# Half rows behind the scores, early splits at the half switch, and M1 in two parts: a hybrid trunk layer on one core

## The chip, the cores and the metric

The kernel runs on one core of one Trainium2 chip. The metric is the device time of one launch in microseconds, given as the median of several runs. Beside it stands one profiled execution, from which all rows below come; their times count from the start of its span.

## What is computed

One layer of a diffusion trunk over 1024 tokens of width 1024, with 256 context tokens that only serve as keys and values. All in fp32:

- a modulation vector `mod = silu(c) @ w_mod + b_mod`, six pieces of 1024: shift, scale and gate of either half layer (`sh1, sc1, g1, sh2, sc2, g2`);
- `h = rms_norm(x) * (1 + sc1) + sh1`, then `h @ w_in`, from which three head groups are made: a chunked gated MLP, attention with 8 query heads over 2 key/value heads (normalised, rotated, 1280 keys), and a gated short convolution;
- `x = x + g1 * (concat(groups) @ w_out)`;
- `x = x + g2 * conv_ffn(rms_norm(x) * (1 + sc2) + sh2)`, where `conv_ffn` is `up = dwconv3(h @ w_up)` (2 × 2816 wide), `silu(g) * a`, and `@ w_down`;
- the output is `rms_norm(x)` times `final_g`.

## The kernel before

Every large product is done on pairs: a number is split into an upper part (`hi`, rounded to fp32r by ScalarE) and a lower part (`lo`, what is left, by VectorE), and three products hi·hi, hi·lo, lo·hi stand for one. A split is therefore one cast on ScalarE and one subtraction on VectorE. A recording layer with engine wrappers makes every instruction, so all of them have one line (L94) in the profile; tiles tell them apart. SP's DMAs keep their written order. The other engines' queues are ordered by a scheduler where `order("")` stands, and as written for the engines named, as `order("TVSG")` in the attention and `order("VS")` at the half switch.

**Attention.** Sixteen units (8 token blocks × 2 key/value heads) are run by a table `PROG`: `a`, `b` are the score products (tile `sl`, two buffers of two PSUM banks), `e` the exponentials on ScalarE, `T` the transpositions of the probabilities (tile `tr`, two banks), `K` and `L` their split (`ph` on ScalarE, `pw` on VectorE), `A` the products with V (`acc`), `f` the copy `sh` on ScalarE, once per unit. Beside it GpSimd multiplies `w_mod` by `silu(c)` for `sh2` and `sc2` and adds up (`mod_macs`, tile `mac`, two buffers, one for each half row of 512 columns). When a half row is done, `head` (L989) lets TensorE sum it over the partitions by four products with `ones` into a `tr` bank, and `tail` (L996) adds the bias on VectorE; both are put into the unit's program at `L8` and `L9`. From unit 16 on, products of the output projection (`po`, `o_early`, L1055) fill TensorE while the last units drain.

**Output projection and the ramp.** For each token block `o_mm` adds the projection to `x1`, `stats2` takes the square sum on ScalarE and `r` by a power on GpSimd and small steps on VectorE, `norm2` makes `xh`. `h_first(kb)` (L1233) transposes `xh` of the first 512 tokens (tile `p2_0*`), ScalarE applies scale and shift (`raw0`), and splits follow (`HB11`, `HB21`). `HF` (L37) says behind which block of the second half which of the eight `kb` are done. The up projection is a Strassen scheme on pairs of weight columns: seven products M1 to M7 on sums of quarter blocks (`HB`, `HT`). `RAMP` (L30) is the written order of its start: M parts of pairs 0 to 2, `H` (transpositions of the second 512 tokens, `p2_1*`), `C` and `F` (the sums), `S` (quarters of M6 and M5).

**Down projection.** It runs over the first 512 tokens, then over the second. For each of 22 `j` one load of gated rows `g` and weights `wd` is split (`d_load`, L1528) and 24 products go to eight `pd` banks. At the half switch `evac` (L1568) multiplies a bank by `g2` on VectorE and GpSimd adds it to `x1`. `final` (L1574) makes the output of a first-half token block at j = 3, 5, 7, 9 of the second half; its two output DMAs stand on SP in front of the next loads. `final_half` (L1586) makes the last block's output in two halves.

## Time and profile before

| | |
|---|---|
| median of 3 runs | 1292.92 us (1291.63 to 1293.93) |
| profiled execution | 1291.2 us, span 1289.4 us |
| mean granted TensorE clock | 0.990 |
| TensorE busy | 1240.2 us, 96% of the span |
| VectorE, ScalarE, GpSimd busy | 955.2, 622.1, 499.3 us |

The busy shares are means over stages with different limits. A row of the timeline gives the start, the duration, the engine, the output and input tiles (numbers left out), how many instructions were merged, and in brackets the idle time before it with what ended that. In the windows view the figure behind the busy times is the granted clock: 1.00 is the 2.4 GHz level, 0.50 the 1.2 GHz level. PE is TensorE, PEld its weight loads, DVE VectorE, ACT ScalarE, POOL GpSimd.

### The profile page before, as it was taken

The numbers are of one execution on the slowest core, as the hardware profiler recorded it, in microseconds if no ns is written. First come the engines' busy times: TensorE is split into PE (matmuls) and PEld (weight loads), VectorE is DVE, ScalarE is ACT, GpSimd is POOL, SyncE is SP. The second block draws the span as 40 slices with busy tenths as digits, with TensorE's granted clock in tenths as the row PEclk, the third lists the DMA queues.
The fourth block names the chain that finished last, engine by engine and source line by source line (L and its number), as shares of the span: only waits on it lengthen the run. The fifth ranks groups of instructions, "written<-read, shape, count | busy, mean of one in ns | idle before, by whom it ended". The sixth has DMA issues, their size and how long they took to land.

```text
span 1289.4 us, 17828 instructions
## 1 busy us (share of the span) xinstructions
PE 1240.2 (96%) x6420; PEld 1031.0 (80%) x6420; DVE 955.2 (74%) x1686; ACT 622.1 (48%) x1126; POOL 499.3 (39%) x497
## 2 busy tenths in 40 slices
PE   6989999999999999999999999999999999999997
PEld 3879899877777778787688888888888888878785
DVE  4797878379899896556999999997778765234545
ACT  4762233368788786225744444444434544122331
POOL 1252243069889855342145453454354110030001
PEclk9999999999999999999999999999999999999999
DMA  9906011111111000811123343333221358023741
GB/s 289 286 18 197 25 34 44 40 50 34 34 65 51 17 2 1 279 70 79 33 82 110 104 131 98 99 114 93 86 83 54 110 211 343 1 98 131 267 173 65
DMA packets 109189, 132.13 MB, mean 102 GB/s; under 512 B 7632, under 2 KB 77998, under 8 KB 109102
## 3 DMA queue, kind: packets, MB, share of 16 engines
q1 hardware_dynamic: 109102, 131.01, 30.9%
q8 instruction: 50, 0.82, 0.3%
q14 instruction: 37, 0.30, 0.1%
HBM read 111.07 MB, written 19.92 MB: 102 GB/s over the span
## 4 chain that ended last, share of the span: by engine, by line
PE 46%; DVE 3%; DMA 2%; ACT 1%; issue 1%; POOL 0%; SPq 0%; POOLq 0%; ACTq 0%; DVEq 0%
PE pd L94 14%; PE pY L94 14%; PE pZ L94 9%; PE pX L94 8%; DMA wd<-in_ffn_down 2%; DVE wd L94 1%; DVE HB L94 1%; DVE x1r L94 1%; SPq L107 0%; DMA x1d<-x 0%; ACT wd L94 0%; ACT HT L94 0%; DMA g<-gud 0%; DVE t_fin L94 0%; DVE xh L94 0%
## 5 line engine op out<-in xcount | busy, mean ns | idle before, releaser
L94 PE MATMUL pd<-wd,gt 128*128 128x512 f32 x912 | 208.4, 390 | 5.1 <-DVE wd L94 4.7
L94 PEld LDWEIGHTS pd<-wd,gt 128*128 128x128 f32 x912 | 171.0, 188 | 42.0 <-DVE wd L94 5.8
L94 PE MATMUL pY<-HT,wM 128*128 128x512 f32 x792 | 192.8, 392 | 2.8 <-ACT HT L94 2.2
L94 PEld LDWEIGHTS pY<-HT,wM 128*128 128x128 f32 x792 | 148.7, 188 | 35.9 <-ACT HT L94 3.3
L94 DVE TENSOR_TENSOR wM<-wu,wM 128x512 fp32r<-128x512 f32 x132 | 133.1, 1012 | 13.7 <-ACT wM L94 13.3
L94 ACT CAST wM<-wu 128x512 fp32r<-128x512 f32 x132 | 80.7, 620 | 114.0 <-PE pY L94 57.2
L94 PE MATMUL pX<-HB,wM 128*128 128x512 f32 x528 | 127.0, 389 | 0.0
L94 DVE TENSOR_TENSOR pw<-tr,ph 128x512 fp32r<-128x512 f32 x160 | 108.2, 682 | 13.0 <-ACT ph L94 11.9
L94 ACT CAST ph<-tr 128x512 fp32r<-128x512 f32 x160 | 93.6, 587 | 47.2 <-PE tr L94 46.0
L94 PEld LDWEIGHTS pX<-HB,wM 128*128 128x128 f32 x528 | 99.0, 188 | 20.4
L94 POOL TENSOR_TENSOR wu<-S,wu 128x512 f32<-128x512 f32 x22 | 29.1, 1322 | 176.5 <-DVE wM L94 176.3
L94 PE MATMUL sl<-K,Q 128*128 128x512 f32 x256 | 83.4, 420 | 1.7 <-ACT pp L94 1.7
L94 DVE TENSOR_REDUCE sm<-sl 128x1 f32<-128x1024 f32 x64 | 77.7, 1216 | 5.3 <-PE sl L94 5.2
L94 PE MATMUL tr<-ident,pp 128*128 128x128 f32 x512 | 78.1, 275 | 1.4
L94 POOL TENSOR_SCALAR pp<-pp,sm 128x1024 f32<-128x1024 f32 x64 | 71.7, 1127 | 17.3 <-DVE sm L94 17.3
L94 PEld LDWEIGHTS tr<-ident,pp 128*128 128x128 f32 x512 | 59.6, 140 | 21.9 <-DVE pw L94 15.5
L94 ACT CAST gt<-g 128x512 fp32r<-128x512 f32 x38 | 23.5, 619 | 110.6 <-DMA g<-gud 79.7
L94 ACT ACTIVATE pp<-sl,sm 128x1024 f32<-128x1024 f32 x64 | 71.5, 1117 | 4.8 <-DVE sm L94 3.8
L94 DVE TENSOR_TENSOR gt<-g,gt 128x512 fp32r<-128x512 f32 x38 | 26.1, 687 | 58.1 <-ACT gt L94 58.1
L94 DVE TENSOR_TENSOR wd<-wd,wd 128x1024 fp32r<-128x1024 f32 x44 | 55.7, 1266 | 17.3 <-ACT wd L94 15.3
L94 PE MATMUL pZ<-HT,wM 128*128 128x512 f32 x264 | 65.1, 393 | 0.3 <-ACT HT L94 0.3
L94 PE MATMUL pZ<-HB,wM 128*128 128x512 f32 x264 | 64.3, 392 | 0.0
(347 smaller groups left out, 2780.5 us busy)
## 6 DMA issues: line engine op xcount, KB each, us to landing
wu<-in_ffn_up SPq DMA_DIRECT2D x88, 256.0 KB, 3.2
wd<-in_ffn_down SPq DMA_DIRECT2D x44, 512.0 KB, 7.4
w<-in_w_mod SPq DMA_DIRECT2D x24, 512.0 KB, 3.7
g<-gud SPq DMA_DIRECT2D x44, 256.0 KB, 5.1
wm<-in_w_mod SPq DMA_DIRECT2D x16, 512.0 KB, 4.6
wi<-in_w_in SPq DMA_DIRECT2D x16, 512.0 KB, 4.7
gud<-y SPq DMA_DIRECT2D x11, 512.0 KB
gud<-ya SPq DMA_DIRECT2D x11, 512.0 KB
```

The lines of the kernel that those rows point to most:

```text
L94: i = fn(*a, **k)
```

## The change

- The 16 products that sum `mac` over the partitions and the four additions behind them are taken out of the attention loop. One `mod_heads` at the start of unit 16 does all 16 products into one `sl` buffer and one addition. `mac` has four buffers.
- `HF` moves each transposition of the first tokens behind a later token block; the last stands behind block 7.
- `RAMP` cuts M1 of pairs 0 and 1 in two parts, as that of pair 2 was, and puts the second parts behind `H0`.
- The first two loads and splits of the second half are written in front of the last `evac` of the first.
- In `final_half` VectorE, not GpSimd, multiplies the first half by `final_g`, the first half's square sum goes into the mean before the second is there, and the two output DMAs are issued by ScalarE and SP.

```diff
@@ -27,14 +27,14 @@
 GLAG = 6
 FINJ = (3, 5, 7, 9)
 GW0 = 4
-RAMP = "M1_0 M1_1 M1_2a H0 M1_2b C0 H1 C1 M2_0 F0 S0 H2 C2 F1 S1 M2_1 H3 C3 S2 S3 M7_0 M7_1 F2 F3"
+RAMP = "M1_0a M1_1a M1_2a H0 M1_0b M1_1b M1_2b C0 H1 C1 M2_0 F0 S0 H2 C2 F1 S1 M2_1 H3 C3 S2 S3 M7_0 M7_1 F2 F3"
 KB = 8
 DFF = 2816
 NF = DFF // P
 QD = 1
 NQ = 1
 PST = 3
-HF = ((0, 1), (2, 3, 4), (5, 6, 7), ())
+HF = ((), (0, 1, 2), (3, 4, 5, 6), (7,))
 SIDE = {2: "a00", 3: "a01", 4: "a20", 5: "a21", 6: "l0", 7: "l1", 8: "w000", 9: "w001",
         10: "w010", 11: "w011", 12: "l2", 13: "l3", 15: "w020"}
 MACS = ("y0", "y1", "z2", "g0")
@@ -143,12 +143,12 @@
     mhalf = const.tile([P, 16], F32, name="mhalf")
     G.memset(mhalf, -0.5)
 
-    def rstd_gen(ss, n, width, pl, name, eng=V):
+    def rstd_gen(ss, n, width, pl, name, eng=V, eps=EPS):
         v = pl.tile([P, width], F32, name=f"v_{name}", tag="rs_v", bufs=4)
         y = pl.tile([P, width], F32, name=f"y_{name}", tag="rs_y", bufs=4)
         t = pl.tile([P, width], F32, name=f"t_{name}", tag="rs_t", bufs=4)
         r = pl.tile([P, width], F32, name=f"r_{name}", tag="rs_r", bufs=4)
-        eng.tensor_scalar(v, ss, 1.0 / n, EPS, ALU.mult, ALU.add)
+        eng.tensor_scalar(v, ss, 1.0 / n, eps, ALU.mult, ALU.add)
         G.tensor_tensor(y, v, mhalf[:, 0:width], ALU.pow)
         yield r
         eng.tensor_tensor(t, v, y, ALU.mult)
@@ -976,7 +976,20 @@
             wos[i] = kq(f"wos{i}", [P, 2, 2, 512])
         fn(wos[i][:, 0, kk, :], wos[i][:, 1, kk, :], wol[i][:, kk, :])
 
-    heads, tails = [], []
+    macc2 = []
+
+    def mod_heads():
+        psb["b1"] = (pst, "sl", 2)
+        pm_ = b1("pm2")
+        for i, ac in enumerate(macc2):
+            for q in range(4):
+                c0 = 8 * i + 2 * q
+                T.matmul(pm_[:, c0:c0 + 2], ac[:, q * P:(q + 1) * P], ones,
+                         start=True, stop=True)
+        b0 = rows["bm"] + 24
+        V.tensor_tensor(mod2[:, 1:3, :].rearrange("p j k -> p (j k)"),
+                        pm_[:, 0:32].rearrange("p (q t) -> p q t", t=2)[:, :, 0],
+                        vT[:, b0:b0 + 16], ALU.add)
 
     def mod_macs(js, acc):
         def load(i):
@@ -985,19 +998,6 @@
             c0 = (2 + j) * D + half * 512
             dma(w_, w_mod[q * 256:(q + 1) * 256, c0:c0 + 512]
                 .rearrange("(k p) n -> p k n", p=P))
-
-        def head(j, half, ac):
-            pm_ = b1(f"pm2_{j}{half}")
-            for q in range(4):
-                T.matmul(pm_[:, 2 * q:2 * q + 2], ac[:, q * P:(q + 1) * P], ones,
-                         start=True, stop=True)
-            tails.append(lambda: tail(j, half, pm_))
-
-        def tail(j, half, pm_):
-            b0 = rows["bm"] + 16 + 8 * j + 4 * half
-            V.tensor_tensor(mod2[:, j, 4 * half:4 * half + 4],
-                            pm_[:, 0:8].rearrange("p (q t) -> p q t", t=2)[:, :, 0],
-                            vT[:, b0:b0 + 4], ALU.add)
 
         ld = {}
         idx = [8 * (j - 1) + i for j in js for i in range(8)]
@@ -1007,6 +1007,7 @@
             j, half, q = i // 8 + 1, i // 4 % 2, i % 4
             if q == 0:
                 ac = acc(f"mac{j}{half}")
+                macc2.append(ac)
             for kk in range(2):
                 k, w_ = 2 * q + kk, ld[i][:, kk, :]
                 G.tensor_scalar(w_ if k else ac, w_, scT[:, k, 0:1], 1.0, ALU.mult, ALU.mult)
@@ -1016,8 +1017,6 @@
                 if kk and n + 2 < len(idx):
                     load(idx[n + 2])
                 yield
-            if q == 3:
-                heads.append(lambda j=j, half=half, ac=ac: head(j, half, ac))
 
     def side(words):
         for w in words.split():
@@ -1125,16 +1124,14 @@
                 sc_, pl = scores(u_ // 2, u_ % 2)
                 us[u_] = {**sc_, **av(u_ // 2, u_ % 2, pl)}
             o, k, l = prog[at]
-            if (o, k) == ("L", 9) and tails:
-                tails.pop(0)()
+            if n == 16 * len(prog):
+                mod_heads()
             if 0 <= u_ - l < 16 and not (u_ == l and o in ops0):
                 us[u_ - l][o](k)
             if u_ == 1 and at == 0:
                 make_gB0()
                 macs = mod_macs((1, 2), lambda nm: tp.tile([P, 512], F32, name=nm, tag="mac",
-                                                              bufs=2))
-            if (o, k) == ("L", 8) and heads and u_ < 16:
-                heads.pop(0)()
+                                                              bufs=4))
             if o + str(k) in MACS:
                 for _ in range(3 if o == "g" and SIDE.get(u_, "l")[0] == "l" else 1):
                     next(macs, None)
@@ -1539,6 +1536,17 @@
     def wd_tile(j, hf):
         return mx(f"wd{j}{hf}", [P, 2, 1024])
 
+    def d_load1(j):
+        if j < NF - LATE:
+            gt = w4(f"gt{j}1", [P, 2, 512])
+        else:
+            if (j - NF + LATE) % 2 == 0:
+                g2.append(ex(f"gl{j}", [P, 2, 2, 512]))
+            gt = g2[-1][:, (j - NF + LATE) % 2]
+        return d_load(j, 1, gt, wd_tile(j, 1))
+
+    g2 = []
+
     def d_load0(j):
         return d_load(j, 0, w4(f"gt{j}0", [P, 2, 512]), wd_tile(j, 0))
 
@@ -1587,16 +1595,18 @@
         sl = x1(7)[:, cs]
         if n2 == 0:
             S.activation(jo[:, 1, cs], sl, AF.Square, accum_out=ss7[:, 0:1])
-            G.tensor_tensor(sl, sl, fg[:, cs], ALU.mult)
+            V.tensor_tensor(sl, sl, fg[:, cs], ALU.mult)
+            V.tensor_scalar(ss7[:, 2:3], ss7[:, 0:1], 1.0 / D, EPS, ALU.mult, ALU.add)
             return
         V.scalar_tensor_tensor(jo[:, 1, cs], sl, 1.0, sl, ALU.mult, ALU.mult,
                                accum_out=ss7[:, 1:2])
-        V.tensor_tensor(ss7[:, 2:3], ss7[:, 0:1], ss7[:, 1:2], ALU.add)
-        r = rstd_from(ss7[:, 2:3], D, 1, xf, "fin7")
+        g = rstd_gen(ss7[:, 1:2], D, 1, xf, "fin7", V, ss7[:, 2:3])
+        r = next(g)
+        next(g, None)
         V.scalar_tensor_tensor(sl, sl, r, fg[:, cs], ALU.mult, ALU.mult)
         S.activation(x1(7)[:, 0:512], x1(7)[:, 0:512], AF.Copy, scale=r)
-        for q in range(2):
-            dma(out[7 * P:8 * P, q * 512:(q + 1) * 512], x1(7)[:, q * 512:(q + 1) * 512])
+        nc.scalar.dma_start(out[7 * P:8 * P, 0:512], x1(7)[:, 0:512])
+        dma(out[7 * P:8 * P, 512:1024], x1(7)[:, 512:1024])
 
     BOTH = [(i, n2) for i in range(4) for n2 in range(2)]
 
@@ -1628,19 +1638,16 @@
             fg = jo[:, 0, :]
             dma(fg, final_g.partition_broadcast(P))
     order("VS")
+    nxt1 = []
     for i, n2 in BOTH:
         for k, ts in enumerate(last):
             d_mm(NF - 4 + k, i, n2, ts)
+        if (i, n2) == (3, 1):
+            nxt1 += [d_load1(0), d_load1(1)]
         evac(i, n2)
     late = []
     for j in range(NF):
-        if j < NF - LATE:
-            gt = w4(f"gt{j}1", [P, 2, 512])
-        else:
-            if (j - NF + LATE) % 2 == 0:
-                g2 = ex(f"gl{j}", [P, 2, 2, 512])
-            gt = g2[:, (j - NF + LATE) % 2]
-        ts = d_load(j, 1, gt, wd_tile(j, 1))
+        ts = nxt1[j] if j < len(nxt1) else d_load1(j)
         if j in FINJ:
             final(FINJ.index(j))
         if j < NF - LATE:
```

On TensorE, where the attention drains (`tr706` transposes probabilities of unit 14, `po00` is the first output projection), stood before:

```order
L94 MATMUL tr706_6171<-ident_67,pp700_5878 128x128 x2
L94 MATMUL tr706_6171<-ident_67,pp702_5973 128x128 x2
L94 MATMUL po00_6182<-wos0_4773,acm00_3591 128x512 x2
L94 MATMUL po00_6182<-wos0_4773,acm01_3592 128x512
L94 MATMUL acc70_6107<-ph704_6146,V_625 128x512
L94 MATMUL acc70_6107<-pw704_6167,V_625 128x512
```

and stands now:

```order
L94 MATMUL tr706_6147<-ident_67,pp700_5855 128x128 x2
L94 MATMUL tr706_6147<-ident_67,pp702_5949 128x128 x2
L94 MATMUL pm2_6158<-ones_96,mac10_3330 128x2 x4
L94 MATMUL pm2_6158<-ones_96,mac11_3921 128x2 x4
L94 MATMUL pm2_6158<-ones_96,mac20_4562 128x2 x4
L94 MATMUL pm2_6158<-ones_96,mac21_5202 128x2 x4
L94 MATMUL po00_6176<-wos0_4761,acm00_3591 128x512 x2
L94 MATMUL po00_6176<-wos0_4761,acm01_3592 128x512
```

All sixteen `pm2` products stand between `tr706` and `po00`.

On TensorE at the start of the ramp (`p2_07` is the last transposition of the first tokens, `p2_10` the first of the second, `pX0` to `pX2` hold M1 of pairs 0 to 2, `po17` before them is the projection of block 7) stood before:

```order
L94 MATMUL pX0_7154<-HB11_0_6954,wM1_0_6744 128x512 x6
L94 MATMUL pX0_7154<-HB11_2_7029,wM1_0_6744 128x512 x6
L94 MATMUL pX1_7169<-HB11_0_6954,wM1_1_6835 128x512 x6
L94 MATMUL pX1_7169<-HB11_2_7029,wM1_1_6835 128x512 x6
L94 MATMUL pX2_7184<-HB11_0_6954,wM1_2_7032 128x512 x6
L94 MATMUL p2_10_7194<-ident_67,xh10_7144 128x128 x2
L94 MATMUL p2_10_7194<-ident_67,xh11_7145 128x128 x2
L94 MATMUL p2_11_7200<-ident_67,xh10_7144 128x128 x2
L94 MATMUL p2_11_7200<-ident_67,xh11_7145 128x128 x2
L94 MATMUL pX2_7184<-HB11_2_7029,wM1_2_7032 128x512 x6
L94 MATMUL p2_12_7231<-ident_67,xh10_7144 128x128 x2
L94 MATMUL p2_12_7231<-ident_67,xh11_7145 128x128 x2
```

and stands now:

```order
L94 MATMUL p2_07_7130<-ident_67,xh01_6892 128x128 x2
L94 MATMUL pX0_7148<-HB11_0_6988,wM1_0_6738 128x512 x6
L94 MATMUL pX1_7155<-HB11_0_6988,wM1_1_6829 128x512 x6
L94 MATMUL pX2_7162<-HB11_0_6988,wM1_2_7008 128x512 x6
L94 MATMUL p2_10_7172<-ident_67,xh10_7138 128x128 x2
L94 MATMUL p2_10_7172<-ident_67,xh11_7139 128x128 x2
L94 MATMUL p2_11_7178<-ident_67,xh10_7138 128x128 x2
L94 MATMUL p2_11_7178<-ident_67,xh11_7139 128x128 x2
L94 MATMUL pX0_7148<-HB11_2_7070,wM1_0_6738 128x512 x6
L94 MATMUL pX1_7155<-HB11_2_7070,wM1_1_6829 128x512 x6
L94 MATMUL pX2_7162<-HB11_2_7070,wM1_2_7008 128x512 x6
L94 MATMUL p2_12_7225<-ident_67,xh10_7138 128x128 x2
```

M1's six products on `HB11_2` of pairs 0 and 1 have moved behind `p2_10` and `p2_11`.

On VectorE at the half switch (`ev` are the evacuations, `gt` and `wd` the lower parts of the splits of the second half) stood before:

```order
L94 TENSOR_TENSOR ev30_11093<-pd30_10405,gacc0_7968 128x512
L94 TENSOR_TENSOR ev31_11108<-pd31_10412,gacc1_8539 128x512
L94 TENSOR_TENSOR gt01_11111<-g01_11113,gt01_11111 128x512
L94 TENSOR_TENSOR wd01_11112<-wd01_11117,wd01_11112 128x1024
L94 TENSOR_TENSOR gt11_11153<-g11_11155,gt11_11153 128x512
L94 TENSOR_TENSOR wd11_11154<-wd11_11159,wd11_11154 128x1024
L94 TENSOR_TENSOR gt21_11187<-g21_11189,gt21_11187 128x512
```

and stands now:

```order
L94 TENSOR_TENSOR ev30_11087<-pd30_10399,gacc0_7962 128x512
L94 TENSOR_TENSOR gt01_11102<-g01_11104,gt01_11102 128x512
L94 TENSOR_TENSOR wd01_11103<-wd01_11108,wd01_11103 128x1024
L94 TENSOR_TENSOR gt11_11112<-g11_11114,gt11_11112 128x512
L94 TENSOR_TENSOR wd11_11113<-wd11_11118,wd11_11113 128x1024
L94 TENSOR_TENSOR ev31_11122<-pd31_10406,gacc1_8533 128x512
L94 TENSOR_TENSOR gt21_11181<-g21_11183,gt21_11181 128x512
```

`ev31` has moved behind the splits of j = 0 and 1.

## Rows read from the trace of the kernel before

**Rows 1.** The page, part 1: busy us (share of the span) and instructions.

```profile
PE 1240.2 (96%) x6420; PEld 1031.0 (80%) x6420; DVE 955.2 (74%) x1686; ACT 622.1 (48%) x1126; POOL 499.3 (39%) x497
```

**Rows 2.** TensorE's waits: tile, releaser, us in total, times, longest.

```profile
PE pm L94 <- DVE pw L94: 5.4, 4, 1.4
...
PE pd L94 <- DVE wd L94: 4.7, 3, 3.2
```

**Rows 3.** Timeline of ScalarE, the copy that each attention unit makes once.

```profile
315.76 0.58 ACT L94 COPY sh<-acc 64x512 f32<-64x512 f32 x1
...
394.03 0.58 ACT L94 COPY sh<-acc 64x512 f32<-64x512 f32 x1
...
408.47 0.58 ACT L94 COPY sh<-acc 64x512 f32<-64x512 f32 x1
...
486.90 0.58 ACT L94 COPY sh<-acc 64x512 f32<-64x512 f32 x1
```

**Rows 4.** Timeline of TensorE at the first of the four sums.

```profile
328.46 1.05 PE L94 MATMUL pm<-ones,mac 128*128 128x2 f32 x8 [1.28 <-DVE pw L94]
329.37 0.71 PE L94 MATMUL sl<-K,Q 128*128 128x512 f32 x2
```

**Rows 5.** Windows: stretch, length, busy by engine, granted clock, DMA share, GB/s.

```profile
331.00:334.00 3.00, 3.00 (x12) 2.40 (x11) 2.00 (x3) 0.97 (x2) 0.80 (x1) 0.50 0.00 0
...
494.00:498.00 4.00, 4.00 (x23) 3.32 (x22) 2.86 (x9) 3.31 (x10) 1.94 (x3) 1.00 0.00 0
...
600.00:700.00 100.00, 96.89 (x431) 78.29 (x430) 89.61 (x119) 56.67 (x89) 33.73 (x19) 0.98 0.23 74
...
620.90:624.20 3.30, 3.30 (x9) 2.55 (x9) 3.30 (x6) 2.25 (x4) 0.00 (x0) 0.51 0.00 0
```

**Rows 6.** Timeline of TensorE at the ramp.

```profile
582.67 0.77 PE L94 MATMUL p<-ident,xh 128*128 128x128 f32 x5 [2.90 <-DVE xh L94]
...
603.98 6.97 PE L94 MATMUL pX<-HB,wM 128*128 128x512 f32 x30
...
619.86 0.50 PE L94 MATMUL pY<-HT,wM 128*128 128x512 f32 x1 [1.92 <-ACT HT L94]
```

**Rows 7.** Timeline of VectorE at the ramp.

```profile
587.76 1.79 DVE L94 TENSOR_TENSOR HB<-raw,HB 128x512 fp32r<-128x512 f32 x1
...
592.75 0.69 DVE L94 TENSOR_TENSOR x<-x,om 128x512 f32<-128x512 f32 x1
...
610.07 0.75 DVE L94 TENSOR_SCALAR xh<-x,r_n 128x1024 f32<-128x1024 f32 x1
```

**Rows 8.** Timeline of ScalarE at the ramp.

```profile
613.28 1.45 ACT L94 ACTIVATE ht<-p,mod,A 128x512 f32<-128x512 f32 x2
...
614.76 0.62 ACT L94 CAST HB<-ht 128x512 fp32r<-128x512 f32 x1
```

**Rows 9.** Timeline of all engines at the half switch and behind it.

```profile
1154.70 0.69 DVE L94 TENSOR_TENSOR ev<-pd,gacc 128x512 f32<-128x512 f32 x1 [2.03 <-PE pd L94]
...
1155.48 1.65 POOL L94 TENSOR_TENSOR x1r<-x1r,ev 128x512 f32<-128x512 f32 x1 [1.43 <-DVE ev L94]
1155.91 2.29 DVE L94 TENSOR_TENSOR wd<-wd,wd 128x1024 fp32r<-128x1024 f32 x1
...
1160.47 1.21 DVE L94 TENSOR_TENSOR wd<-wd,wd 128x1024 fp32r<-128x1024 f32 x1
...
1163.34 0.14 DVE L94 TENSOR_SCALAR v_fin<-ssf 128x1 f32<-128x1 f32 x1
...
1215.22 0.96 PE L94 MATMUL pd<-wd,gt 128*128 128x512 f32 x3 [0.76 <-DVE wd L94]
```

**Rows 10.** Timeline of GpSimd, VectorE and SP at the end.

```profile
1280.43 1.26 POOL L94 TENSOR_TENSOR x1r<-x1r,jo 128x512 f32<-128x512 f32 x1 [4.44 <-ACT jo L94]
1280.60 0.69 DVE L94 TENSOR_TENSOR ev<-pd,gacc 128x512 f32<-128x512 f32 x1 [1.07 <-PE pd L94]
...
1285.73 0.81 SPq L107 DMA_DIRECT2D out_x<-x1r  x2
```

## The prediction

> **What bounds the kernel now.** I read the page first, then TensorE's waits, then the timeline at each place that the change touches, then the granted clock in small windows. TensorE is busy 96% of the span [rows 1], so the change can only pay where TensorE stands still, runs at the lower clock, or is held back by VectorE. Two lines of its waits carry what the change aims at: four waits of the `pm` products, together 5.4 us, and three of `pd`, together 4.7, the longest 3.2 [rows 2].
>
> The attention stage has to be read by its period, not by that line. ScalarE's `sh` copy comes once per unit. Between two units without `pm` products the period is 408.47 − 394.03 = 14.44 us; eleven periods, among them all four with `pm` products, take 486.90 − 315.76 = 171.14 [rows 3]. That is 171.14 − 11 × 14.44 = 12.3 us over the plain period, more than twice the 5.4 that the waits show. The rest is seen at the first of the four: TensorE waits 1.28 us for a `tr` bank, then spends 0.91 us (328.46 to 329.37) on eight records of two columns [rows 4], and after it the granted clock is 0.50, the 1.2 GHz level, for 3 us [rows 5].
>
> Behind the attention the bound is TensorE itself (4.00 of 4.00 us busy at 494 to 498, VectorE 2.86 [rows 5]). In the ramp of the channel mixer TensorE waits 2.90 us for the last `xh` of the first half and 1.92 us for the first `HT` tile [rows 6]; VectorE is busy 89.61 of 100 us there and the clock is 0.51 behind the second of these waits [rows 5]. What VectorE does between these two places is in [rows 7], ScalarE's pieces in [rows 8], the half switch in [rows 9], the tail in [rows 10].
>
> **The change part by part.**
>
> *Products of the second modulation vector.* Sixteen products leave the attention loop, four at a time, and stand together behind `tr706`. What goes are the 12.3 us: without them nothing takes a `tr` bank out of turn, and the plain period is what the twelve other units show. Nothing else becomes late: the accumulators get four buffers instead of two, so GpSimd waits for no product either. What comes: 4 × 0.91 = 3.6 us of products, then an addition on VectorE before the bank is free; for which I take 0.3, a short operation with its two signals. `po00`, the next in TensorE's queue, so begins about 3.9 us later. VectorE has `pw705` behind the addition, and ScalarE and GpSimd wait for that; all of it moves by the same 3.9 us, since TensorE is the bound there. Bounds: 3.6 if the addition hides, 5 if the bank has to wait as each of the four did. And the clock: after 1.28 us of waiting and 0.91 us of two-column products it fell; here some 4 us of such work stand in a row, so I take a fall: 3 to 3.3 us at half speed, 1.6 us. Sum of this part: −12.3 + 3.9 + 1.6 = −6.8 us.
>
> *First tokens' transpositions one block later, M1 in two parts.* The wait of 2.90 us goes: `xh` of the fourth token block is there long before `po15` ends. But it was not on the path. From 592.75, where `x1` of block 5 is added, to 610.07, where `xh` of block 7 starts [rows 7], the order is set by VectorE and ScalarE: each block's addition stands in VectorE's queue behind the `xh` of the block before, which waits for square sum, power and three small steps. TensorE has no wait in these 17 us; it is fed ahead. The move takes two `HB` subtractions out of the link to block 5 and puts one more into the link to block 7. One such subtraction took 1.79 us beside GpSimd's additions. Bounds for `xh` of block 7: at most 2 × 1.79 − 0.7 = 2.9 us earlier, at least 0. The subtractions gone, `xh` of block 4 itself falls beside these additions, so I take 0.9: it starts at 609.2 and is done at 609.9.
>
> TensorE meanwhile runs ahead: `po15` follows at once, and it is through `po17`, `p2_07` and the first parts of M1 (18 products, 4.2 us at 6.97/30 each [rows 6]) by about 603.5. Then it stands at the fourth piece of `p2_10`, which needs that `xh`, for some 6 us, with the second parts of M1 queued behind it. Before, M1 stood there whole and ended just as `xh` was ready (603.98 + 6.8 = 610.8). So the wait is not removed but moved, from a place with cover to one without: 18 products (4.2 us, against 6 before, 1.4 us) are now behind `xh`, and the first 3.2 us of them at half clock (+1.6). They end near 616.4. From there ScalarE has the last M1 copy and two transposed rows (0.7 each) and six pieces of 0.62 [rows 8] before M6 has its first tile, and the copy waits a further 0.9 for a buffer that VectorE frees: 616.4 + 2.1 + 3.7 + 0.9 = 623.1, against 619.86 [rows 6], 3.2 us late. Of this I give 1.4 back: before, the clock was at 0.51 for 3.3 us behind M6's wait [rows 5], which cost TensorE up to 1.6; now the fall has come earlier, and M2 of the second pair is two products further. Sum: +1.8. Bounds: −1 (the 2.9 us come, no fall) and +4 (no gain for `xh`, a fall at both places).
>
> *Early splits at the half switch.* Before, VectorE did `ev31` at 1154.70, then `gt01` and `wd01` (2.29 us beside GpSimd's addition of 1.65), and TensorE waited 3.21 of the 4.7 us. Now the four splits stand in front of `ev31`; the first can start behind `ev30` at about 1152.7, `wd01` is done near 1155.7, and TensorE's first six products need only the upper parts, which ScalarE has ready by then. `ev31` ends near 1158.4, before its bank's turn, 21 products after 1155.05, at 1159.8. So these 3.2 us go. What is late next is the chain of loads: `v_fin` of the first final block at 1163.34 is the head of a round of statistics, output, loads and splits, every two j, that is slower than TensorE; at 1215.22, in j = 10, TensorE waited 0.76 us for it [rows 9]. This chain starts where VectorE is through eight splits and `ev31`, the same 8.6 us of work (1154.70 to 1163.34) from 1152.7 on, plus one more collision with GpSimd, 1.08 us (2.29 less the 1.21 of an undisturbed one): 1162.4, 0.9 us earlier. From j = 8 on TensorE is paced by it, so of the 3.2 us 0.9 stay; and as the upper products now stand first at j = 8 and 10, the wait of 0.76 and the product in front of it hide, 1.0 us. Sum: −1.9. Bounds: 0 (the chain doesn't move) and −4.7 (all three waits go [rows 2]).
>
> The collision is where a page can be weighed. The wide split took 2.29 us beside GpSimd's 1.65 us addition [rows 9]. The Trainium skill (SBUF — State Buffer, "SBUF: two separate sides") says that a VectorE operation with two inputs in SBUF and a GpSimd operation that reads it exclude each other for a whole instruction. The trace agrees: the split took 1.08 us longer than its like, most of the rest of that addition. By that rule the early splits meet two such additions, `ev30`'s and `ev31`'s, and the part is the −1.9; without it −3.0.
>
> *Tail.* VectorE now multiplies by `fg`, behind ScalarE's square (done when GpSimd started at 1280.43) and in front of `ev71`, which started at 1280.60 [rows 10]. A product of this size takes it 0.69 us, as `ev71` does, so with the small step behind it `ev71` starts near 1281.3, 0.7 later. Back come the collision with GpSimd's product and one small step, together about as much as two small steps (0.3), and half of the two issues that took 0.81 us in a row on SP (0.4). Sum: 0 us, between −0.4 and +0.8 (nothing back; a first issue on ScalarE's queue isn't in this trace).
>
> The Trainium skill (DMA: Bandwidth & Descriptors, "Issuing engines are not separate DMA queues") says that a second issuing engine saves only issue time; by it the saving is the same 0.4 and no more.
>
> Sum: −6.8 + 1.8 − 1.9 + 0 = −6.9. The profiled execution took 1291.2 (span 1289.4 and 1.8 around it), so 1284.3 for its like. The median of the runs shown, 1292.92, lies 1.7 above it: 1286.0.
>
> **The rivals.** (a) *All waits go*: the ramp gives its 2.90 and 1.92, the switch 3.2, the products bring no fall: −12.3 + 3.9 − 4.8 − 3.2 = −16.4, 1276.5. For it: the waits stand on TensorE, the busiest engine. Against: the chain to block 7's `xh`, which has no TensorE wait in it. (b) *Gain eaten*: attention as forecast, but the chain of loads doesn't move and the ramp takes its upper bound: −6.8 + 4 + 0 = −2.8, 1290.1. For it: both chains are slower than TensorE. Against: `ev31` is shown to hold VectorE at 1154.70. (c) *Slower*: the ramp. If the rows behind `xh` come so late that VectorE, 89.61 of 100 us busy there [rows 5], has the splits of the next two pairs ready after their turn, TensorE waits at each of their eight steps; 1 us each and the +4 make +12: −6.8 + 12 − 1.9 = +3.3, 1296.2. It decides from a ramp loss of 11.3 us on, 8.7 for the other parts' gain and 2.6 beyond. Against it: in all of TensorE's waits none of that size lies between 619.86 and the half switch. (d) *The heads' time isn't free*: the plain period grows by what GpSimd has left from the pauses, half of the 12.3: −6.9 + 6.2 = −0.7, 1292.2. Against: plain periods keep 14.44 wherever two follow each other.
>
> **How the numbers follow.** Forecast 0.66, with its own range 1282 to 1289.5; (a) 0.12; (b) 0.12; (d) 0.06; (c) 0.04. The range runs from 1280.5, into (a), whose middle cases count, to 1290.3. A measurement of this kernel tells 0.2% (2.6 us) from no change: below 1290.3 lie the forecast, (a), and most of (b): 0.87; within it the rest of (b), and (d): 0.09; above it (c): 0.04.
>
> **What would show it.** Right: all periods of `sh` up to the fourteenth unit at 14.4 us; about 3.6 us of `pm` products near 481 with a low clock behind them; no wait at the first `p2` rows, one of 5 to 6 us in front of block 7's piece of `p2_10` and low clock on M1's second parts; no wait at the first `pd` of the second half, waits of 1 to 2 us at j = 8 and 10. Wrong: periods over 15 us; a wait under 3 us in front of `p2_10`, or M6 earlier against the `po` products before it than now; no wait at all in the second half.

## The result and the profile after

The changed kernel took 1281.01 us (1279.75 to 1281.82, median of 4 runs) against 1292.28 in the same set; the ratio is 0.9921, with a 95% interval of 0.9902 to 0.9940. A second set gave 1278.81 against 1291.53, ratio 0.9909 (0.9895 to 0.9923). The two intervals have gains of 10 to 12.7 us in common; 6.9 was forecast. The profiled execution took 1281.82, with a span of 1280.0 (1289.4 before).

The page's part 1, against [rows 1]:

```profile
PE 1236.4 (97%) x6420; PEld 1029.6 (80%) x6420; DVE 959.3 (75%) x1684; ACT 622.1 (49%) x1126; POOL 497.4 (39%) x496
```

TensorE does the same 6420 instructions; it is idle 5.6 us less and busy 3.8 us less. Of the 3.8, some 1.8 are clock, by an estimate that takes half of its busy time at the 1.2 GHz level as lost (10.2 us in the trace before, 8.3 in this one). Its waits (tile, releaser, us in total, times, longest), against [rows 2]:

```profile
PE p L94 <- DVE xh L94: 5.8, 1, 5.8
...
PE pd L94 <- ACT wd L94: 2.7, 2, 1.8
...
PE pZ L94 <- ACT wM L94: 0.8, 1, 0.8
...
PE po L94 <- DVE mod L94: 0.3, 1, 0.3
```

The four `pm` waits of 5.4 us are gone. The wait for `xh` has doubled, and `pd` has lost the long one.

**Attention.** The same copies on ScalarE's timeline as in [rows 3], and then TensorE's timeline at the drain:

```profile
316.17 0.58 ACT L94 COPY sh<-acc 64x512 f32<-64x512 f32 x1
...
474.81 0.58 ACT L94 COPY sh<-acc 64x512 f32<-64x512 f32 x1
```

```profile
481.65 3.78 PE L94 MATMUL pm<-ones,mac 128*128 128x2 f32 x32
485.69 1.65 PE L94 MATMUL po<-wos,acm 128*128 128x512 f32 x3 [0.27 <-DVE mod L94]
```

Eleven periods now take 474.81 − 316.17 = 158.64, 14.42 each, where they took 171.14: 12.5 us are gone. They were the four waits (5.4), the products themselves (4 × 0.91) and two stretches of low clock (some 1.7 each). The sixteen products with the wait for their addition hold `po00` for 485.69 − 481.65 = 4.04. Behind them the windows view (length, busy by engine, granted clock) shows the 1.2 GHz level:

```profile
481.00:485.00 4.00, 4.00 (x37) 3.90 (x35) 1.18 (x2) 1.96 (x6) 1.25 (x2) 1.00 0.00 0
485.00:491.50 6.50, 6.23 (x19) 4.98 (x19) 2.26 (x8) 1.65 (x4) 1.58 (x2) 0.50 0.00 0
```

TensorE is busy in both rows; in the second it does in 6.5 us what takes about half as long at 1.00, so some 3.3 us are lost, twice my 1.6. The fall comes at 485.0, ahead of the 0.27 us wait that ends at 485.69. So the products and the clock come back here, and of the 12.5 us the waits are what stays gone.

**Ramp.** TensorE's timeline, against [rows 6], a row of the windows view, and the last `xh` on VectorE's timeline, against [rows 7]:

```profile
604.24 1.33 PE L94 MATMUL p<-ident,xh 128*128 128x128 f32 x5 [5.78 <-DVE xh L94]
605.22 5.58 PE L94 MATMUL pX<-HB,wM 128*128 128x512 f32 x18
...
615.95 0.50 PE L94 MATMUL pY<-HT,wM 128*128 128x512 f32 x1
```

```profile
604.20:607.60 3.40, 3.37 (x11) 2.89 (x12) 0.68 (x1) 2.06 (x3) 0.00 (x0) 0.50 0.02 5
```

```profile
599.22 0.68 DVE L94 TENSOR_TENSOR om<-po,gB 128x512 f32<-128x512 f32 x1
...
603.43 0.75 DVE L94 TENSOR_SCALAR xh<-x,r_n 128x1024 f32<-128x1024 f32 x1
```

The wait has moved to block 7's piece of `p2_10`, and the 18 products of M1's second parts behind it take 5.58 us (the clock is 0.50 from 601 to 607.9). M6 follows without a wait, and no low clock follows it. ScalarE's timeline in front of it, against [rows 8], has the last transposed rows and then six pieces at 0.52 each, the last of which releases M6:

```profile
611.32 1.46 ACT L94 ACTIVATE hta<-p,mod,A 128x512 f32<-128x512 f32 x2
...
615.27 0.62 ACT L94 CAST HT<-ht 128x512 fp32r<-128x512 f32 x1
```

In VectorE's first row above, the eviction `om` of `po17` begins 5.8 us after TensorE is through that block's `po` products (593.4).

**Half switch.** `ev30` on VectorE's timeline, first before and then now, then VectorE's and TensorE's timeline behind it, against [rows 9]:

```profile
1151.98 0.69 DVE L94 TENSOR_TENSOR ev<-pd,gacc 128x512 f32<-128x512 f32 x1 [2.03 <-PE pd L94]
```

```profile
1145.71 0.69 DVE L94 TENSOR_TENSOR ev<-pd,gacc 128x512 f32<-128x512 f32 x1 [2.03 <-PE pd L94]
...
1146.92 2.32 DVE L94 TENSOR_TENSOR wd<-wd,wd 128x1024 fp32r<-128x1024 f32 x1
...
1150.90 0.68 DVE L94 TENSOR_TENSOR ev<-pd,gacc 128x512 f32<-128x512 f32 x1
...
1152.10 2.31 DVE L94 TENSOR_TENSOR wd<-wd,wd 128x1024 fp32r<-128x1024 f32 x1
...
1156.07 0.14 DVE L94 TENSOR_SCALAR v_fin<-ssf 128x1 f32<-128x1 f32 x1
```

```profile
1143.63 48.22 PE L94 MATMUL pd<-wd,gt 128*128 128x512 f32 x212
1192.80 11.17 PE L94 MATMUL pd<-wd,gt 128*128 128x512 f32 x48 [0.95 <-ACT wd L94]
1205.72 8.48 PE L94 MATMUL pd<-wd,gt 128*128 128x512 f32 x36 [1.75 <-ACT wd L94]
```

TensorE runs through the switch. The head of the load chain, `v_fin`, comes 10.36 us behind `ev30` (1145.71), where it was 11.36 behind (1151.98): 1.0 earlier. Two waits are left, 0.95 and 1.75, as forecast. Two of the early splits take 2.3 us, each beside one of GpSimd's additions (1.67 us from 1146.48 and 1.68 from 1151.65). By the rule weighed in the prediction (the Trainium skill, SBUF — State Buffer, "SBUF: two separate sides") there should be just two such collisions; the trace agrees.

**Tail.** VectorE's timeline, against [rows 10]:

```profile
1271.14 0.69 DVE L94 TENSOR_TENSOR x1r<-x1r,jo 128x512 f32<-128x512 f32 x1 [0.85 <-ACT jo L94]
...
1271.81 0.68 DVE L94 TENSOR_TENSOR ev<-pd,gacc 128x512 f32<-128x512 f32 x1
```

The product stands in front of `ev71`, which starts 0.5 us behind TensorE's end (1271.31) instead of with it.

**Three stretches for all traces.** One pair of traces is not enough, since the clock's falls and the waits of the second half differ from execution to execution of one kernel. So all traces of this study are cut at four marks: first and last `sh` copy, `ev30`, and TensorE's end.

| trace | `sh` to `sh` | `sh` to `ev30` | `ev30` to end of TensorE |
|---|---|---|---|
| before / r9_before2 | 231.05 / 232.72 | 634.30 / 634.55 | 128.59 / 128.40 |
| r11_ramp_on_before | 231.28 | 633.84 | 128.64 |
| after / r10_after2 | 225.33 / 223.95 | 633.36 / 634.26 | 125.60 / 123.90 |
| r1_oldramp | 225.34 | 632.26 | 127.15 |
| r2_hfonly | 225.37 | 630.77 | 124.10 |
| r3_spread | 221.66 | 633.65 | 124.62 |
| r4_latesplit | 225.39 | 633.12 | 126.82 |
| r5_pipe | 224.02 | 629.19 | 126.33 |
| r6_actout | 225.42 | 633.06 | 122.28 |
| r7_dummy | 225.38 | 636.17 | 125.21 |
| r8_combo | 221.69 | 627.83 | 124.52 |
| r12_all | 221.62 | 627.83 | 122.29 |

Means over the traces with the same code in a stretch: attention 231.68 (3 traces) to 225.03 (8), −6.7. Ramp 634.43 (2) to 633.55 (6), −0.9. Half switch 128.11 (4) to 125.18 (8), −2.9. The tail, from TensorE's end to the span's, went from 8.85 (3 traces) to 8.7, −0.15. The sum is −10.6, inside what the two ratios allow.

### The profile page after: what moved, and what is told of

Its sections match the earlier page's. It is cut to its first block, busy times and chain, and to the rows that moved or that the text cites. A ratio compares the mean times of both kernels' runs of the same rounds, so it can differ in the third digit from the quotient of the medians.

```text
span 1280.0 us, 17818 instructions
## 1 busy us (share of the span) xinstructions
PE 1236.4 (97%) x6420; PEld 1029.6 (80%) x6420; DVE 959.3 (75%) x1684; ACT 622.1 (49%) x1126; POOL 497.4 (39%) x496
## 4 chain that ended last, share of the span: by engine, by line
PE 64%; DVE 22%; DMA 4%; issue 4%; POOL 3%; ACT 3%; SPq 1%; POOLq 0%; DVEq 0%; ACTq 0%
PE pY L94 14%; PE pd L94 14%; PE pZ L94 9%; PE pX L94 8%; DVE sm L94 8%; DVE pw L94 6%; PE pq L94 3%; PE po L94 2%; DMA wd<-in_ffn_down 2%; PE pau L94 2%; PE pcc L94 2%; PE pcb L94 2%; PE pav L94 2%; PE pch L94 2%; PE pm L94 1%
## 5 line engine op out<-in xcount | busy, mean ns | idle before, releaser
L94 DVE TENSOR_TENSOR wM<-wu,wM 128x512 fp32r<-128x512 f32 x132 | 138.8, 1056 | 12.4 <-ACT wM L94 12.2
```

Of the source, the lines that this page charges most:

```text
L94: i = fn(*a, **k)
```

## The experiments

The edits stand against the changed kernel, except for r9_before2 and r11_ramp_on_before. Each kernel was timed against the kernel before in 5 rounds. The changed kernel's ratio to it is 0.9921 (0.9902 to 0.9940) and 0.9909 (0.9895 to 0.9923), so a single edit that moves the total by 3 or 4 us is hardly clear of these intervals. For single edits the argument rests on the stretches of the table, one trace each; the totals of the combinations are clear.

**The ramp taken back**

```diff
-RAMP = "M1_0a M1_1a M1_2a H0 M1_0b M1_1b M1_2b C0 H1 C1 M2_0 F0 S0 H2 C2 F1 S1 M2_1 H3 C3 S2 S3 M7_0 M7_1 F2 F3"
+RAMP = "M1_0 M1_1 M1_2a H0 M1_2b C0 H1 C1 M2_0 F0 S0 H2 C2 F1 S1 M2_1 H3 C3 S2 S3 M7_0 M7_1 F2 F3"
-HF = ((), (0, 1, 2), (3, 4, 5, 6), (7,))
+HF = ((0, 1), (2, 3, 4), (5, 6, 7), ())
```

> The changed kernel with the ramp of before (first tokens' transpositions one block earlier, M1 of pairs 0 and 1 in one piece), all else as changed. Theory (read from the two traces): the new ramp gave 0.8 us, because the clock fell once instead of twice and the 1.9 us wait at M6 went, against 1.5 us of later start; so this kernel takes 0.5 to 1.5 us more than the changed one, 1281.5 to 1282.5 in the median, with a 2.9 us wait back at the first p2 rows and one of about 2 us at M6. Rival (as I had forecast): the new ramp costs 1.8 us and the gain came from elsewhere; then this kernel is 1.8 us faster, 1279.

1281.01 (1277.38 to 1283.10), ratio 0.9918 (0.9898 to 0.9938), the same as with the new ramp. The 2.9 us wait is back, but M6's is 1.3 instead of 1.9, and no low clock follows it. The ramp's stretch is 1.3 us shorter than with the new ramp (632.26 against 633.55), so in these surroundings the new ramp costs by this one trace, as the rival said. The time doesn't show it; in the profiled execution the clock fell behind the last wait of the second half (1204.6 to 1208.1), and whether it does so in the other runs isn't known.

**Transpositions late, M1 whole** (only the line `RAMP` taken back)

> The changed kernel with M1 of pairs 0 and 1 in one piece again, the later transpositions kept. Theory: what costs in the new ramp are the products queued behind the xh of block 7 (18, at half clock, 5.6 us). With M1 whole, 12 of them stand in front of the wait; the wait shrinks from 5.8 to about 3 us, only 6 products stand behind, and M6 starts 2 to 3.5 us earlier: 1277.5 to 1279.5. Rival: M6 is held by ScalarE's and VectorE's chain behind the transposed rows, not by these products; then M6 starts at the same time and the median stays within 0.5 us of 1281.

1277.96 (1274.88 to 1278.53), ratio 0.9890 (0.9870 to 0.9910). TensorE's timeline:

```profile
599.58 4.84 PE L94 MATMUL pX<-HB,wM 128*128 128x512 f32 x20 [0.69 <-DVE HB L94]
604.26 0.49 PE L94 MATMUL p<-ident,xh 128*128 128x128 f32 x3
605.07 0.77 PE L94 MATMUL p<-ident,xh 128*128 128x128 f32 x5 [0.33 <-DVE xh L94]
605.59 1.62 PE L94 MATMUL pX<-HB,wM 128*128 128x512 f32 x6
```

M1 fills the time before `xh`, and of the 5.78 us wait 0.33 is left (with 1.8 in front of M1's later products). M6 starts 100.1 us behind the last `sh`, 3.5 earlier than in the changed kernel (103.6), and the stretch is 2.8 us under the mean of the new ramp. Of the two edits to the ramp the later transpositions gain (1.5 us against r1_oldramp) and the division of M1 costs (2.8), by one trace each of r1_oldramp and r2_hfonly.

**The sixteen products spread**

```diff
-        pm_ = b1("pm2")
+        both_ = b1("po00", 1024)
+        po1[0, 0] = both_[:, 0:512]
+        pm_ = both_[:, 512:1024]
+        yield
         for i, ac in enumerate(macc2):
             for q in range(4):
                 c0 = 8 * i + 2 * q
                 T.matmul(pm_[:, c0:c0 + 2], ac[:, q * P:(q + 1) * P], ones,
                          start=True, stop=True)
+                yield
...
+            if u_ >= 16 and (o in OSLOT or (o in "TA" and u_ - l < 16)):
+                next(heads2, None)
```

> The changed kernel, with the 16 two-column products spread singly between the transpositions, acc and po products of the drain instead of in one row (same products, same addition). Theory: the row of two-column products is what pulls the clock to 0.50 for 6.6 us, which costs 3.3; spread, the clock stays at 1.00 and the wait of 0.27 goes; the 3.8 us of the products themselves stay. So 3 to 3.5 us less: 1277.5 to 1278. Rival: the products cost the same wherever they stand, because the fall has another cause (the end of the attention's denser work); then the low stretch is still there and the time is within 0.5 us of 1281.

1276.71 (1275.96 to 1279.62), ratio 0.9894 (0.9875 to 0.9913). Three rows of TensorE's timeline, then the windows view of the drain:

```profile
481.58 0.28 PE L94 MATMUL po<-ones,mac 128*128 128x2 f32 x2
481.71 0.48 PE L94 MATMUL acc<-ph,V 128*128 128x512 f32 x1
482.03 0.39 PE L94 MATMUL acc<-pw,V 128*128 128x512 f32 x1
```

```profile
479.00:495.00 16.00, 16.00 (x105) 14.10 (x105) 8.93 (x24) 8.62 (x18) 12.05 (x15) 1.00 0.01 2
```

The same products leave the clock at 1.00, and the attention's stretch loses 225.37 (r2_hfonly, the same drain with the long fall) − 221.66 = 3.7 us: 3.4 of clock (half of 6.9 us), 0.27 of wait. The products themselves got no cheaper. In r8_combo and r12_all it is the same (221.69, 221.62). The fall follows the row in eight traces of eight and is missing in the three where the products are spread: that the products in one row bring it is shown.

**Late splits**

```diff
         if (i, n2) == (3, 1):
-            nxt1 += [d_load1(0), d_load1(1)]
+            pass
```

> The changed kernel with the splits of j = 0 and 1 behind the last eviction again. Theory: the half switch gave 3.0 us, of which 2.4 are in the waits; so 2.4 to 3.2 us more than the changed kernel, 1283.5 to 1284.2, with the wait of 3.2 us back and the first v_fin 1.0 us later against ev30. Rival: the load chain paces anyway and half of the gain is noise between two profiles; then at most 1.5 us more.

1283.84 (1282.02 to 1284.47). The wait of 3.21 is back, and one of 0.71 behind it; `v_fin` comes 11.35 us behind `ev30`, 1.0 later, as the theory says. The stretch, 126.82, is 1.2 over the first trace of the changed kernel and 1.6 over the mean with early splits, near the rival's bound of 1.5. The ratio to the kernel before is 0.9941 (0.9924 to 0.9958), 2.6 to 4.1 us more than the changed kernel's two, which is the theory's size. The stretch is short in this trace since the later waits are 0.71 us in all (1.87 in the first trace of the kernel before) and no low clock follows the long one; the mean of the four traces with late splits is 128.11.

**VectorE's order in the ramp**

```diff
+    order("V")
     for tb in range(4, 8):
         o_mm(1, tb)
-        stats2(tb)
...
+        S.activation(jk, x1(tb), AF.Square, accum_out=ss2[:, tb:tb + 1])
+        if tb > 4:
+            chain2(tb - 1)
...
+    chain2(7)
+    order("")
```

`chain2` is the power chain and the `xh` of one block.

> The changed kernel with VectorE's order in the ramp turned: the eviction and addition of the next block stand in front of the power chain and xh of the block before (the same operations, pinned in that order). Theory: the xh of block 7 is late because po17's eviction stands in VectorE's queue behind xh of block 6, 5.8 us after TensorE is done with it; with the eviction first, xh of block 7 comes at about 598 instead of 603.4, the wait of 5.8 us and the low clock behind it go, and the stretch from the last sh copy to the last evictions of the first half shrinks by 4 to 6 us: 1275 to 1277. Rival: VectorE is the bound in the ramp as a whole; what is moved ahead delays the splits of the first tokens, and the stretch shrinks by less than 1.5 us.

1277.26 (1276.14 to 1280.86), ratio 0.9904 (0.9886 to 0.9922). VectorE's timeline:

```profile
592.83 0.69 DVE L94 TENSOR_TENSOR om<-po,gB 128x512 f32<-128x512 f32 x1
...
595.74 0.75 DVE L94 TENSOR_SCALAR xh<-x,r_n 128x1024 f32<-128x1024 f32 x1
...
599.13 0.75 DVE L94 TENSOR_SCALAR xh<-x,r_n 128x1024 f32<-128x1024 f32 x1
```

The eviction now stands ahead of `xh` of block 6, `xh` of block 7 comes 88.8 us behind the last `sh` instead of 91.1, TensorE waits 2.2 us instead of 5.8, and the clock stays at 1.00 through the ramp. The stretch loses 4.4 us against the mean. This order set some 3.6 of the 5.8 us; what sets the other 2.2 isn't shown.

**Final outputs on ScalarE's queue**

```diff
-            dma(out[tb * P:(tb + 1) * P, cs], x1(tb)[:, cs])
+            (nc.scalar.dma_start if tb < 4 else dma)(out[tb * P:(tb + 1) * P, cs], x1(tb)[:, cs])
```

> The changed kernel, with the output transfers of the four final blocks in the second half issued on ScalarE's queue instead of SP's. Theory: the loads stand in SP's queue behind these outputs, which wait for VectorE's final products, and that paces the second half; with the outputs on the other queue the loads start earlier, the pd waits at j = 8 and 10 (0.95 and 1.75 us) go and the stretch from ev30 to TensorE's end falls from 125.6 to about 122.9: 1278 to 1278.5. Rival: the loads wait for free buffers rather than for the outputs, and ScalarE's casts now stand behind the issue: the waits stay or grow, 1281 to 1283.

1277.97 (1277.00 to 1279.51), ratio 0.9905 (0.9887 to 0.9922). TensorE's timeline of the second half has one row without a wait up to the last tiles:

```profile
1139.80 94.00 PE L94 MATMUL pd<-wd,gt 128*128 128x512 f32 x414
1233.64 32.80 PE L94 MATMUL pd<-wd,gl 128*128 128x512 f32 x144
```

The heads of the four final blocks, `v_fin`, now follow each other by 8 us (1154.68, 1162.69, 1170.63, 1178.58), where in the changed kernel they came every 13 to 14 (1156.07, 1168.91, 1182.83, 1195.91). The stretch is 122.28, and 122.29 in r12_all. The loads had been held by the outputs ahead of them in SP's queue, as that queue's timeline of the changed kernel shows:

```profile
1158.43 1.00 SPq L107 DMA_DIRECT2D out_x<-x1r  x2
1159.52 0.41 SPq L107 DMA_DIRECT2D g<-gud  x1
...
1171.27 1.00 SPq L107 DMA_DIRECT2D out_x<-x1r  x2
1172.38 0.40 SPq L107 DMA_DIRECT2D g<-gud  x1
```

Two pairs of loads go out right behind each pair of outputs, and none until the next pair 13 us later. The Trainium skill (DMA: Bandwidth & Descriptors, "Issuing engines are not separate DMA queues") says that a second issuing engine saves only the time of the issue; here the stretch lost 2.9 us against the mean, since what stood in the queue was an issue that waits for VectorE.

**Work in the wait**

```diff
             if (hf, kb, i) == (1, 0, 3):
+                for r in range(44):
+                    T.transpose(pt[:, 3 * P:4 * P], xs[6][:, 0:P], ident)
```

> The changed kernel with 44 more transpositions of a finished row, written to the place in p2_10 that block 7's piece overwrites, in front of that piece; they fill the 5.8 us in which TensorE waits there. Theory: the wait itself is set by VectorE's chain and stays, but the clock no longer falls, so the 18 products of M1's second parts take 4.2 instead of 5.6 us and M6 starts 1.4 us earlier: 1279 to 1280. Rival: M6 is held by the rows and casts behind xh of block 7 on ScalarE, and the faster products change nothing: 1281, or up to 0.5 more if the dummies outlast the wait.

1284.76 (1281.78 to 1287.07), ratio 0.9955 (0.9938 to 0.9973): slower than the changed kernel. TensorE's timeline:

```profile
600.17 5.29 PE L94 MATMUL p<-ident,xh 128*128 128x128 f32 x47
606.46 0.77 PE L94 MATMUL p<-ident,xh 128*128 128x128 f32 x5 [1.00 <-DVE xh L94]
606.98 4.34 PE L94 MATMUL pX<-HB,wM 128*128 128x512 f32 x18
...
636.60 7.37 PE L94 MATMUL pY<-HT,wM 128*128 128x512 f32 x24 [1.51 <-DVE u L94]
```

The first step came as the theory said: the 18 products take 4.34 us, and M6 starts 101.95 us behind the last `sh` instead of 103.6. But the longer TensorE queue also changed the order of ScalarE's and VectorE's splits behind it, where nothing pins it; a wait of 1.51 for `u` and a fall of the clock (636.7 to 640.1) follow, and the stretch is 2.6 longer than the mean. The total says nothing on the clock's term.

**Three together**: spread, M1 whole, VectorE's order

> Spread products, M1 in one piece, and VectorE's turned order, together on the changed kernel. If the three work at different places: -3.7 (drain) and, in the ramp, what the turned order leaves of the 2.6 that M1 in one piece gave; the wait that this one hid is gone then, so I take -5 for both together: 1272. If the ramp is bound by VectorE as a whole: 1274 to 1275.

1271.99 (1270.96 to 1274.94), ratio to the kernel before 0.9861 (0.9842 to 0.9880). The ramp's stretch is 627.83, 5.7 under the mean of the new ramp.

**Both kernels again, and the ramp alone on the kernel before**

> The kernel before once more, for a second trace of it. The ramp change looks worth 0.9 us when the two first traces are compared (stretch from the last sh copy to the last evictions of the first half 634.3 against 633.4), but -1.1 when the old ramp stands in the changed kernel (632.3). If the low clock behind M6 (621 to 624) and the 3.2 + 1.9 us of waits at the half switch belong to this kernel, they are here again and the stretch is 634 to 634.5; if they vary from execution to execution, the stretch without the low clock is 632 to 633.

> The changed kernel once more, for a second trace. The low clock behind the 16 products (6.6 us) and from 601 to 607.6 should be here again, since the work in front of them is the same in each execution: attention stretch 225.3 to 225.4, the stretch to the evictions 633.1 to 633.7, from there to TensorE's end 124 to 125.6, depending on the waits at j = 8 and 10, which varied between 1.0 and 2.7 us in the runs with the early splits.

> The kernel before with the new ramp alone (later transpositions, M1 in two parts). Theory: in surroundings of its own the new ramp costs about 1 us against an old one without the low clock behind M6 and gains 1 us against one with it: stretch from the last sh copy to the evictions 633.1 to 633.7, time within 1 us of the kernel before. Rival (my forecast before the result): 1.8 us slower, stretch 636.

Before again: 1291.48, and its ramp 634.55, with the low clock behind M6 (623.7 to 627.2) again. After again: 1278.81; its low stretch behind the sixteen products lasted from 484.5 to 488.0 only, and its attention is 1.4 us shorter. The new ramp alone on the kernel before: 1290.53 (1288.85 to 1294.39), ratio 0.9998 (0.9987 to 1.0009), no change; its stretch is 633.84.

The two traces with the old half switch show something that the first did not. The windows view of r9_before2 around the 3.21 us wait, which ends at 1160.80:

```profile
1160.00:1166.00 6.00, 5.20 (x12) 4.13 (x13) 6.00 (x8) 3.29 (x5) 0.00 (x0) 0.50 0.05 17
```

The first trace had 1.00 there. Yet the stretch is the same (128.40 and 128.59), as the later waits (1.87 us in the first trace) are missing here: TensorE is slower, and the loads are ready when it comes. This fits a stretch that is paced by its loads, which r6_actout bears out.

**All four together**

> Spread products, M1 in one piece, VectorE's turned order, and the final outputs on ScalarE's queue, together on the changed kernel. The first three took 1272.0 together; the outputs on ScalarE's queue took the waits of the second half away alone, 3.3 us there, of which the first three leave 2.2 (124.5 against 122.3 from ev30 to TensorE's end): 1269.5 to 1270. If the faster loads collide with the rest of the second half when TensorE comes earlier: 1271 to 1272.

1268.64 (1268.36 to 1268.93), ratio to the kernel before 0.9826 (0.9812 to 0.9840), against 1278.81 for the changed kernel in the same set. It is the fastest version here.

## Why the prediction was right, and where a term was off

*Products of the second modulation vector: −6.8 forecast, −6.7 measured on the means.* The 12.3 that I took from the period came as 12.5 [rows 3], and the 3.9 for `po00` as 4.04. The clock's 1.6 was mis-sized: some 3.4 in six of eight traces, 1.7 in two. That the sum still agrees is in part luck: from the first two traces alone it is −5.7, and the kernel before lost 1.7 us to the low clock two, three and two times in the attention of its three traces. Sorted by kind, 5.1 of the 6.7 us are TensorE's waits (5.7 to 0.5), about 1.0 is clock (4.0 to 3.0 on the means), and the other 0.5 isn't traced. So the net gain came out near the 5.4 of the waits [rows 2] after all, since the products and most of the clock's price only moved. The four `mac` buffers and the new place of the products were not tried apart.

*Ramp: +1.8 forecast, −0.9 measured between the stretches. This term carries 2.7 of the 3.7 us by which the sum was short.* The mechanism is there: the wait of 2.90 gone, one of 5.8 (some 6 forecast) at block 7's piece, `xh` 1.3 earlier against the last `sh` (0.9), 18 products behind it that took 5.58 us (4.2 + 1.6 forecast). The step that failed is "they end near 616.4 ... 616.4 + 2.1 + 3.7 + 0.9 = 623.1, ... 3.2 us late". From the end of the second parts to M6 it took 5.3 us (610.63, where the next transpositions start, to 615.95), not 6.7: the 0.9 for a buffer that VectorE frees didn't come (VectorE itself stood idle for ScalarE for 1.6 us, until 609.24), and the six pieces of ScalarE followed each other by 0.52, not 0.62. M6 starts 1.5 late (103.8 against 102.3 behind the last `sh`, means of 6 and 2 traces). And from M6 to `ev30` 2.4 us came back, where I gave 1.4: 532.1 (1151.98 − 619.86) against 529.8 (1145.71 − 615.95); the low clock is some 1.6 of it, by an estimate from 3.3 us at 0.51. Between these traces the sign of the term came out wrong because both halves erred to the same side, 1.7 and 1.0. As an edit alone the ramp moved no total: r11_ramp_on_before has the ratio 0.9998 (0.9987 to 1.0009), which leaves no room for +1.8, and r1_oldramp the median of the changed kernel. Its stretch gives +1.3 in the changed kernel, where the old ramp has no fall behind M6 (one trace), so the sign of the new ramp's effect seems to go with that fall; this is argued from one trace, not shown.

*Half switch: −1.9 forecast, −2.9 measured (−2.4 in the waits of the first pair).* The chain's head moved by 1.0 (0.9 forecast), the collisions and the two left waits are as forecast in the first trace (four of the eight traces with early splits have only one of the waits). With the same code the stretch lies between 123.9 and 127.15. On the means the waits over 0.2 us fall by 2.0 (3.9 to 1.8), close to the forecast; low clock, which the forecast had put at nothing here, stands in two of the four traces with late splits (6.9 us each) and in two of the eight with early ones (3.5 each). r6_actout shows the chain's cause and its price, 2.9 more.

*Tail: 0 forecast, −0.15 measured.* VectorE's product delayed `ev71` by 0.5 instead of 0.7; its three edits were not tried apart.

Of the rivals, (d) falls by the periods of 14.42, (b) by `v_fin`, (c) by the lack of any wait over 1 us between M6 and the switch; (a) holds for the switch's long wait only. The range, 1280.5 to 1290.3, holds the time of the first set, 0.5 us above its lower end; the second set's 1278.81 lies below it. With the ramp's sign wrong, that the first came out inside is luck as well.

## What to carry to other kernels

Where work is inserted into a periodic loop, its price is the lengthened period: the waits that the profile books on it, the work itself, and the low clock behind it. Put elsewhere, the work and perhaps the clock come back, so price both places the same way. Where small products are put together, let them stand between full ones, not in a row. When a wait moves instead of going, price the whole way to the next place where TensorE is the bound, with the waits and low clocks that vanish there, and look in the in-order queue of the engine that ends it for an older instruction to let pass. A transfer that waits for a result doesn't belong in the queue that also issues the loads.

## What was not expected of the hardware

- The same sixteen products were followed by 6.9 us of granted clock 0.50 in six traces and by 3.5 us in two (r5_pipe, r10_after2).
- M6's waits of 1.92 and 2.14 us were followed by a fall, those of 1.31 and 1.32 (r1_oldramp, r2_hfonly) were not. The half switch's wait of 3.21 us was followed by one in r9_before2 and r11_ramp_on_before, not in the first trace nor in r4_latesplit. Why M6's wait is shorter when the old ramp stands in the changed kernel stays open.
- A two-column product cost the same in both places. In the row the 16 took 3.78 us, 0.24 each. Spread, one pushed the next full product back by 0.13 us (481.58 to 481.71), and that product then held TensorE for 0.32 (481.71 to 482.03) where its neighbour behind took 0.23 (482.03 to 482.26): 0.22 together.
